# Two blocks in float32 on one core: where the first mixer's tables, weight splits and rotations stand

## The chip, the core and the metric

The kernel runs on one core of a Trainium2 chip. The core's engines each work through a queue of their own in order: TensorE (PE; its weight loads are PEld), VectorE (DVE), ScalarE (ACT), GpSimd (POOL) and SyncE (SP, which here only starts transfers). Semaphores tie the queues together. The metric is the device time of one execution in microseconds (us), and the number to compare is the median over the runs of a kernel.

## What is computed

256 tokens of width 1024 go in float32 through two blocks. The first is feed-forward, attention, feed-forward, each with a norm ahead of it and one behind it; the second has two layers, each a mixer and a feed-forward part.

```
x = x + 0.5 * rmsnorm(swiglu(rmsnorm(x, pre), gate, up, down), post)      # part f1
x = x + rmsnorm(attention(rmsnorm(x, mix_pre)) @ w_out, mix_post)         # part m1, the first mixer
x = x + 0.5 * rmsnorm(swiglu(...), post)                                  # part f2
x = x + ab_mixer(rms_norm(x));  x = x + swiglu(rms_norm(x), ...)          # parts ab, f3
x = x + cd_mixer(rms_norm(x));  x = x + swiglu(rms_norm(x), ...)          # parts cd, f4
return rms_norm(x)
```

The attention of m1 has 8 heads of one kind (group A, two key heads shared by four query heads each, their queries and keys normed per head) and 8 of another (group B). In both, each 64-wide head of queries and keys is rotated: `out = q * cos + swapped(q) * sin`. In group A the norm's gain is multiplied into the cosine and sine tables (`cg`, `sg`), so the rotation is two multiplications, an addition and a multiplication by the norm's `r`.

## The kernel before

**Products.** Each float32 product is made of three fp32r products: an operand is split in a high part (a cast) and a low part (the operand less the cast). Weights come in tiles of 128x1024 (512 KB). `Stream` keeps four raw tiles (`wraw`) and six split ones (`wh`, `wl`): SP starts the load, ACT casts `wraw` to `wh` (L89), and DVE or POOL subtracts to get `wl` (L94). The load of the tile four further on waits until that subtraction is done, since the raw buffer is free only then, and the cast of the tile six further on waits until PE has used the tile. `take` splits ahead to six tiles. Which engine subtracts is written in the code: `ws.pool = (1,)` sends every second tile of a stretch to POOL; empty, all go to DVE.

**Order.** Nothing is reordered: each engine's queue is the order of the program text. `bg` is a list of small pieces of work that `pump` takes from within the products.

**Entry to a part.** `enter` (called by each part but the first through its own) closes the part before for the two halves of 128 tokens, h = 0 and then h = 1: `ew` adds the result to `x` (L406 where there is a norm behind, L409 otherwise), computes the norm of the new `x` (squares on ACT, L336; the power -1/2 on POOL, L344 and L346) and scales it to `xs` (L423). `to_t` transposes `xs` on PE (`tp`, L370), casts it on ACT (`xt`, L373) and subtracts on DVE (`xt`, L378). Two weight tiles are cast and subtracted on the way; the second, `split[1]`, is subtracted on POOL. `first` is the first product, for h = 0 and then h = 1; the transposes of h = 1 stand inside the product of h = 0 (`mid`).

**The first mixer.** `mixer1` makes, in this order on PE: the queries of group A (`gh`), its keys and values (`gemm_a256`, 48 short products, `ga`), the first half of group B's `qb` (`gemm_a`, four tiles, `ga`), then `gemm_a` again with pieces between its tiles: after the second tile the transposes (`tq`, L790) of group A's rotated keys (chunk 4 of `ra`) and of some queries, after the third the other queries, after the fourth the first logits (`step(0)`). A third `gemm_a` has `step(1)` to `step(4)` between its tiles. `step(i)` does the logits of head i (`lg`), the softmax of head i-1 (exponentials on ACT, sum's reciprocal `ls` on DVE, L840, multiplication of `e` by it on POOL, L841), the transposes of head i-3's `e` (`pT`, L849) and the product with the values of head i-4 (`o`).

Behind `gh`, POOL loads `rope`, `gqk` and the mask, makes `cg` and `sg` (L729, eight instructions) and clears `va` and `vb` (L733, four). `rope_a(h)` then does group A's rotation for 10 heads of half h (8 of queries, 2 of keys) in five pieces, with the norm's power on POOL (`rra`, L751). `rope_b(h, eng)` rotates group B's 16 heads of half h in four instructions in a row, for h = 0 on POOL and for h = 1 on DVE (L777, L780 twice, L782):

```
self.ws.pool = (1,)
bank = self.gemm_a()
...
self.flush()
self.ws.pool = ()
bank = self.gemm_a({1: lambda: tr(raf, qta, ((4,), (0, 1))), 2: ..., 3: lambda: step(0)})
...
rope_b(0, nc.gpsimd)
rope_b(1, nc.vector)
```

Of the kernel before, what the change touches and what calls it, by code (L numbers as in the profile page):

```python
# [8 lines left out]
F32 = mybir.dt.float32  # L9
# [22 lines left out]
HH_AT = (352, 352, 96, 352)  # L32
# [156 lines left out]
class Kern:  # L189
# [266 lines left out]
    def enter(self, gname, first):  # L456
# [236 lines left out]

    def mixer1(self, gnext):
        nc, A = self.nc, self.A
        tt = nc.vector.tensor_tensor
        with ExitStack() as st:
# [25 lines left out]
            nc.gpsimd.dma_start(out=rope, in_=A["c_rope"])  # L723
            nc.gpsimd.dma_start(out=gqk, in_=A["gqk"].partition_broadcast(P))
            nc.gpsimd.dma_start(out=mask, in_=A["c_maskb"])
            for h in range(2):
                for tab, i in ((cg, 0), (sg, 1)):
                    for (a, b, g) in ((0, 8, i), (8, 10, 2 + i)):
                        nc.gpsimd.tensor_tensor(  # L729
                            out=tab[:, h, a:b, :], in0=rope[:, h, i:i + 1, :].to_broadcast([P, b - a, 64]),  # L730
                            in1=gqk[:, g:g + 1, :].to_broadcast([P, b - a, 64]), op=ALU.mult)
            for t in va + vb:
                nc.gpsimd.memset(t.bitcast(F32), 0.0)  # L733
            kv = self.gemm_a256()
            for h in range(2):
                nc.vector.tensor_copy(out=fl(qa[:, h, 8:10, :]), in_=kv[:, h, 0:128])
                src = kv[:, h, 128:256].rearrange("p (a w) -> p a w", a=2)
                nc.scalar.copy(out=va[0][:, h, :, 1, :], in_=src)
                tt(out=va[1][:, h, :, 1, :], in0=src, in1=va[0][:, h, :, 1, :].bitcast(F32), op=ALU.subtract)

            def rope_a(h):
                t1 = ap.tile([P, 10, 64], F32, name="t1", tag="pp", bufs=2)
                t2 = ap.tile([P, 10, 64], F32, name="t2", tag="pp", bufs=2)
# [30 lines left out]
            def rope_b(h, eng):
                t2 = ap.tile([P, 16, 64], F32, name="t3", tag="pp", bufs=2)
                cc = rope[:, h, 2:3, :].to_broadcast([P, 16, 64])
                eng.tensor_tensor(out=rb[:, h], in0=qb[:, h], in1=cc, op=ALU.mult)  # L777
                for y in range(2):
                    a, b = slice(32 * y, 32 * y + 32), slice(32 - 32 * y, 64 - 32 * y)
                    eng.tensor_tensor(out=t2[:, :, a], in0=qb[:, h, :, b],  # L780
                                      in1=rope[:, h, 3:4, a].to_broadcast([P, 16, 32]), op=ALU.mult)
                eng.tensor_tensor(out=rb[:, h], in0=rb[:, h], in1=t2, op=ALU.add)  # L782
# [954 lines left out]
```

## Time and profile before

| | before |
| --- | --- |
| median of 3 runs (lowest to highest) | 1124.01 us (1123.45 to 1124.99) |
| the profiled execution | 1124.95 us, of which 1123.2 us are its span |
| busy: PE, PEld | 1094.8 us (97%), 926.4 us |
| busy: DVE, ACT, POOL | 743.5 us (66%), 598.9 us, 357.3 us |
| DMA | 190.83 MB, mean 170 GB/s |

The parts lie in the span about as follows: f1 to 197 us, m1 to 323, f2 to 509, ab to 631, f3 to 826, cd to 932, f4 to the end. The list of PE's waits names who ended an idle stretch of PE; the chain of waits goes back from the last instruction to what released each step; a timeline row gives start, duration, engine, line, operation, output and inputs, and in square brackets the idle time ahead of it and who ended it. A row with xN merges N like instructions in a row.

### The profile page before, as it was taken

The page shows a single profiled execution, that of the slowest core. Times are in us where ns is not written, and L with a number is a line of the kernel's source. Part 1 is how long each engine was busy: PE and PEld are TensorE (multiplying, and loading weights), DVE is VectorE, ACT ScalarE, POOL GpSimd, SP SyncE. Part 2 cuts the span into 40 slices and gives each one's busy share as a digit, 9 for nine tenths or more (in the row PEclk, how much of TensorE's full clock was granted, in tenths as well). Part 3 has the DMA queues.
Part 4 walks back from the last instruction along what each step waited for, and adds up shares of the span by engine and source line. Part 5 has one row for each costly group of instructions (what it writes and reads, how often), then busy time and mean ns, then how long its engine had stood idle before and what let it go on. Part 6 is the DMA issues. An engine that isn't in the chain of part 4 may idle for free.

```text
span 1123.2 us, 16090 instructions
## 1 busy us (share of the span) xinstructions
PE 1094.8 (97%) x5963; PEld 926.4 (82%) x5963; DVE 743.5 (66%) x988; ACT 598.9 (53%) x954; POOL 357.3 (32%) x572
## 2 busy tenths in 40 slices
PE   8999999989999999999989999999999999999997
PEld 5888888767878888887976888888889888888886
DVE  5666566789676665667573677667777656656664
ACT  4567555545655454555664555545452465554553
POOL 2006700655320000004151499999624221000000
PEclk9999999989999999999988999999999999999999
DMA  7765655652047656655621565565554326655651
GB/s 229 251 199 166 209 188 187 211 169 76 20 153 223 201 175 200 211 171 178 204 90 38 187 199 175 190 187 155 183 177 151 131 86 203 196 191 188 215 167 69
DMA packets 130256, 190.83 MB, mean 170 GB/s; under 512 B 6017, under 2 KB 101249, under 8 KB 130178
## 3 DMA queue, kind: packets, MB, share of 16 engines
q1 hardware_dynamic: 129440, 187.72, 52.3%
q0 software_dynamic: 736, 2.08, 0.6%
q8 instruction: 47, 0.77, 0.3%
q14 instruction: 31, 0.25, 0.1%
q10 hardware_dynamic: 2, 0.00, 0.0%
HBM read 188.73 MB, written 1.05 MB: 169 GB/s over the span
## 4 chain that ended last, share of the span: by engine, by line
PE 84%; DVE 6%; POOL 3%; issue 2%; ACT 2%; DMA 1%; SPq 0%; POOLq 0%; DVEq 0%; ACTq 0%
PE gb L535 26%; PE f L523 21%; PE gb L537 13%; PE wo L523 4%; PE gb L523 4%; PE fh L642 3%; PE gh L523 2%; PE ga L523 1%; PE o L869 1%; PE lg L523 1%; PE lt L1100 1%; DVE x L406 1%; DMA wraw<-in_w_first_dram 1%; PE pT L849 1%; PE tp L370 1%
## 5 line engine op out<-in xcount | busy, mean ns | idle before, releaser
L94 DVE TENSOR_TENSOR wl<-wraw,wh 128x1024 fp32r<-128x1024 f32 x323 | 394.0, 1261 | 111.2 <-ACT wh L89 110.7
L535 PE MATMUL gb<-xt,wh 128*128 128x512 f32 x1280 | 439.1, 390 | 0.0
L89 ACT CAST wh<-wraw 128x1024 fp32r<-128x1024 f32 x341 | 345.0, 1047 | 58.1 <-PE f L523 11.4
L537 PE MATMUL gb<-xt,wl 128*128 128x256 f32 x1280 | 353.9, 277 | 0.0
L535 PEld LDWEIGHTS gb<-xt,wh 128*128 128x128 f32 x1280 | 240.3, 188 | 50.6
L537 PEld LDWEIGHTS gb<-xt,wl 128*128 128x128 f32 x1280 | 240.5, 188 | 1.7
L523 PE MATMUL f<-wh,hh 128*128 128x512 f32 x348 | 138.2, 397 | 0.0
L523 PE MATMUL f<-wh,hl 128*128 128x512 f32 x348 | 137.1, 394 | 0.0
L523 PE MATMUL f<-wl,hh 128*128 128x512 f32 x348 | 136.9, 393 | 0.0
L659 ACT COPY sg<-gb 128x256 f32<-128x256 f32 x80 | 29.8, 373 | 140.5 <-PE gb L537 137.2
L660 DVE TENSOR_TENSOR sg<-gb,sg 128x256 f32<-128x256 f32 x80 | 33.4, 423 | 94.4 <-ACT sg L659 94.2
L94 POOL TENSOR_TENSOR wl<-wraw,wh 128x1024 fp32r<-128x1024 f32 x21 | 58.6, 2803 | 86.5 <-ACT wh L89 83.8
L344 POOL TENSOR_TENSOR v<-ss 128x1 f32<-128x1 f32 x22 | 6.2, 281 | 242.0 <-ACT xs L336 180.7
L339 POOL TENSOR_SCALAR ss<-ss 128x1 f32<-128x1 f32 x6 | 2.5, 409 | 244.7 <-ACT xs L336 244.7
L523 PEld LDWEIGHTS f<-wh,hl 128*128 128x128 f32 x348 | 65.3, 188 | 16.8 <-DVE hl L654 0.9
L523 PEld LDWEIGHTS f<-wh,hh 128*128 128x128 f32 x348 | 65.4, 188 | 14.6
L523 PEld LDWEIGHTS f<-wl,hh 128*128 128x128 f32 x348 | 65.4, 188 | 13.3
L523 PE MATMUL gb<-xt,wh 128*128 128x256 f32 x384 | 69.1, 282 | 0.0
L659 ACT COPY su<-gb 128x256 f32<-128x256 f32 x80 | 29.2, 368 | 64.7 <-PE gb L537 64.7
L523 PEld LDWEIGHTS gb<-xt,wh 128*128 128x128 f32 x384 | 59.4, 188 | 0.4
L523 PE MATMUL gb<-xt,wl 128*128 128x256 f32 x192 | 54.3, 283 | 0.0
L523 PE MATMUL wo<-wh,xt 128*128 128x512 f32 x160 | 52.6, 400 | 0.0
(406 smaller groups left out, 1641.9 us busy)
## 6 DMA issues: line engine op xcount, KB each, us to landing
wraw<-in_ffn_w_down_dram SPq DMA_DIRECT2D x88, 512.0 KB, 3.8
wraw<-in_ffn_w_gate_dram SPq DMA_DIRECT2D x80, 512.0 KB, 4.1
wraw<-in_ffn_w_up_dram SPq DMA_DIRECT2D x80, 512.0 KB, 5.6
wraw<-in_ab_w_in_dram SPq DMA_DIRECT2D x20, 512.0 KB, 4.8
wraw<-in_w_qkv_dram SPq DMA_DIRECT2D x18, 512.0 KB, 3.8
wraw<-in_w_first_dram SPq DMA_DIRECT2D x16, 512.0 KB, 3.9
wraw<-in_cd_w_in_dram SPq DMA_DIRECT2D x16, 512.0 KB, 4.5
wraw<-in_w_out_dram SPq DMA_DIRECT2D x8, 512.0 KB, 4.2
```

Of the source, the lines that this page charges most:

```text
L89: self.nc.scalar.copy(out=h, in_=r)
L94: eng.tensor_tensor(out=l, in0=r, in1=h.bitcast(F32), op=ALU.subtract)
L370: nc.tensor.transpose(p[:, j * P:(j + 1) * P], src[:, (b + j) * P:(b + j + 1) * P], self.ident)
L406: nc.vector.scalar_tensor_tensor(out=xv[:, c], in0=t[:, c], scalar=r, in1=xv[:, c], op0=ALU.mult, op1=ALU.add)
L523: self.nc.tensor.matmul(out=out, lhsT=l, rhs=r, start=start and i == 0, stop=stop and i == n - 1)
L535: self.nc.tensor.matmul(out=p, lhsT=wh[:, k % 4, c], rhs=self.x2[:, k, :], start=k == 0, stop=False, skip_group_check=True)
L537: self.nc.tensor.matmul(out=p[:, S:2 * S], lhsT=wl[:, k % 4, c], rhs=self.xh[:, k, :], start=False, stop=k == 7, skip_group_check=True)
L642: nc.tensor.matmul(out=p, lhsT=l, rhs=r, start=n == 0, stop=n == 23)
L659: nc.scalar.copy(out=t[:, c, :], in_=p[:, 1, :])
L660: tt(out=t[:, c, :], in0=p[:, 0, :], in1=t[:, c, :], op=ALU.add)
L849: nc.tensor.transpose(p[:, k * S + h * P:k * S + (h + 1) * P], e[:, h, k * P:(k + 1) * P], self.ident)
L869: nc.tensor.matmul(out=o, lhsT=v, rhs=p, start=i % 2 == 0 and n == 0, stop=i % 2 == 1 and n == 5)
```

## The change

- `enter`: `split[1]` is subtracted on DVE and no longer on POOL, and it stands behind the second `next(e1)` (the update of `x` for h = 1) in place of ahead of the transposes.
- The tiles `rope`, `gqk`, `maskb`, `cg`, `sg`, `va`, `vb` get a pool of their own, opened ahead of f1 and closed behind m1 (`m1_open`). `m1_load` (loads and clears) is hooked to step 5 of f1, `m1_tables(0)` and `m1_tables(1)` to steps 8 and 9. `va` is 5 wide in place of 2x3, with the values at places 1 and 3. Gaps of bytes (`HH_AT`, `gap`) place the tiles.
- `rope_a(h, heads)` takes a slice of the heads: h = 0's eight query heads are rotated at once behind `enter`, ahead of the keys' product; h = 1's eight queries, then the two keys of h = 0 and of h = 1, three pieces each, go through `bg` in the first `gemm_a`.
- `ws.pool` stays empty: no weight tile of the first `gemm_a` is subtracted on POOL.
- `rope_b` runs on DVE for both halves, in four pieces each through `bg` in the third `gemm_a`.

```diff
-HH_AT = (352, 352, 96, 352)
+HH_AT = (512, 352, 96, 352)
...
         next(e1)
-        split[1](nc.gpsimd)
         self.new_xt()
         low = self.to_t(0, xs, self.xh, self.xl)
         next(e1)
+        split[1](nc.vector)
         low()
...
+    def m1_load(self):
+        nc, A = self.nc, self.A
+        nc.gpsimd.dma_start(out=self.rope, in_=A["c_rope"])
+        nc.gpsimd.dma_start(out=self.gqk, in_=A["gqk"].partition_broadcast(P))
+        nc.gpsimd.dma_start(out=self.maskb, in_=A["c_maskb"])
+        for t in self.va + self.vb:
+            nc.gpsimd.memset(t.bitcast(F32), 0.0)
+
+    def m1_tables(self, h):
+        for tab, i in ((self.cg, 0), (self.sg, 1)):
+            for (a, b, g) in ((0, 8, i), (8, 10, 2 + i)):
+                self.nc.gpsimd.tensor_tensor(
...
-            nc.gpsimd.dma_start(out=rope, in_=A["c_rope"])
...
-            for t in va + vb:
-                nc.gpsimd.memset(t.bitcast(F32), 0.0)
...
+            for f in rope_a(0, slice(0, 8)):
+                f()
             kv = self.gemm_a256()
...
-            self.bg += rope_a(0) + rope_a(1)
-            self.pump(3)
+            self.bg += rope_a(1, slice(0, 8)) + rope_a(0, slice(8, 10)) + rope_a(1, slice(8, 10))
...
-            self.ws.pool = (1,)
             bank = self.gemm_a()
...
-            self.ws.pool = ()
...
-            rope_b(0, nc.gpsimd)
-            rope_b(1, nc.vector)
+            self.bg += rope_b(0) + rope_b(1)
...
+                hooks = {j: [step(a), step(b)] for j in (2, 4, 6)} if i == 0 else {}
+                self.m1_open(stm)
+                hooks.update({5: [self.m1_load], 8: [lambda: self.m1_tables(0)], 9: [lambda: self.m1_tables(1)]})
+                self.ffn(pre, "ffn1_post_g", 0.5, nxt, hooks)
```

PE, ACT and SP have the same instructions in the same order as before; DVE's and POOL's queues change. Three places:

DVE at the entry to m1, before, from the scaled `xs` of h = 0 to the low part of h = 1:

```order
L423 SCALAR_TENSOR_TENSOR xs<-x,r,g_mix_pre_g 128x512 x2
L401 TENSOR_TENSOR pt<-f_411,g_ffn_post_g 128x512
L401 TENSOR_TENSOR pt<-f_412,g_ffn_post_g 128x512
L406 SCALAR_TENSOR_TENSOR x<-pt,r,x 128x512 x2
L378 TENSOR_TENSOR xt<-tp,xt 128x4x128 x2
L423 SCALAR_TENSOR_TENSOR xs<-x,r,g_mix_pre_g 128x512 x2
```

The same stretch of DVE now:

```order
L423 SCALAR_TENSOR_TENSOR xs<-x,r,g_mix_pre_g 128x512 x2
L401 TENSOR_TENSOR pt<-f_424,g_ffn_post_g 128x512
L401 TENSOR_TENSOR pt<-f_425,g_ffn_post_g 128x512
L406 SCALAR_TENSOR_TENSOR x<-pt,r,x 128x512 x2
L94 TENSOR_TENSOR wl<-wraw,wh 128x1024
L378 TENSOR_TENSOR xt<-tp,xt 128x4x128 x2
L423 SCALAR_TENSOR_TENSOR xs<-x,r,g_mix_pre_g 128x512 x2
```

One weight subtraction has come between the update of `x` and the low part; the five other entries change in the same way.

DVE ahead of the first transposes `tq` (the low part `qtal` is the first work behind them), before; `t_...` are the rotation's scratch tiles, `ssa` the sums of squares:

```order
L765 TENSOR_TENSOR ra<-t_2178,rra 128x2x4x64
L769 TENSOR_TENSOR ra<-t_2178,rra 128x128
L748 TENSOR_TENSOR t_2184<-qa 128x640
L749 TENSOR_REDUCE ssa<-t_2184 128x10
L754 TENSOR_TENSOR t_2183<-qa,cg 128x640
L94 TENSOR_TENSOR wl<-wraw,wh 128x1024
L758 TENSOR_TENSOR t_2184<-qa,sg 128x20x16 x2
L762 TENSOR_TENSOR t_2183<-t_2183,t_2184 128x640
L765 TENSOR_TENSOR ra<-t_2183,rra 128x2x4x64
L769 TENSOR_TENSOR ra<-t_2183,rra 128x128
L94 TENSOR_TENSOR wl<-wraw,wh 128x1024 x2
L796 TENSOR_TENSOR qtal<-tq,qtah 128x256
```

And now:

```order
L773 TENSOR_TENSOR ra<-t_2254,rra 128x128
L94 TENSOR_TENSOR wl<-wraw,wh 128x1024
L754 TENSOR_TENSOR t_2305<-qa 128x128
L755 TENSOR_REDUCE ssa<-t_2305 128x2
L760 TENSOR_TENSOR t_2304<-qa,cg 128x128
L762 TENSOR_TENSOR t_2305<-qa,sg 128x4x16 x2
L767 TENSOR_TENSOR t_2304<-t_2304,t_2305 128x128
L773 TENSOR_TENSOR ra<-t_2304,rra 128x128
L94 TENSOR_TENSOR wl<-wraw,wh 128x1024 x2
L816 TENSOR_TENSOR qtal<-tq,qtah 128x256
```

What stands last ahead of the transposes is now the rotation of two key heads of h = 1, where it was that of all ten heads of h = 1.

POOL in the same stretch and up to the first multiplications of `e`, before:

```order
L750 TENSOR_SCALAR vva<-ssa 128x10
L751 TENSOR_TENSOR rra<-vva,mhalf 128x10
L94 TENSOR_TENSOR wl<-wraw,wh 128x1024 x2
L750 TENSOR_SCALAR vva<-ssa 128x10
L751 TENSOR_TENSOR rra<-vva,mhalf 128x10
L94 TENSOR_TENSOR wl<-wraw,wh 128x1024
L777 TENSOR_TENSOR rb<-qb,rope 128x1024
L780 TENSOR_TENSOR t_2396<-qb,rope 128x16x32 x2
L782 TENSOR_TENSOR rb<-rb,t_2396 128x1024
L841 TENSOR_TENSOR e<-e,ls 128x512 x8
```

And now:

```order
L756 TENSOR_SCALAR vva<-ssa 128x8
L757 TENSOR_TENSOR rra<-vva,mhalf 128x8
L756 TENSOR_SCALAR vva<-ssa 128x8
L757 TENSOR_TENSOR rra<-vva,mhalf 128x8
L756 TENSOR_SCALAR vva<-ssa 128x2
L757 TENSOR_TENSOR rra<-vva,mhalf 128x2
L756 TENSOR_SCALAR vva<-ssa 128x2
L757 TENSOR_TENSOR rra<-vva,mhalf 128x2
L860 TENSOR_TENSOR e<-e,ls 128x512 x8
```

POOL's three weight subtractions and its half of group B's rotation are gone from here. Its loads and clears (L708 to L712) now follow at the program's start directly on the power of h = 1's first norm (L346), and the eight table instructions (L717) on the last of the small preparations of part f1.

## Rows read from the trace of the kernel before

**Rows 1.** PE's waits: who waited for whom, us in total, times, longest.
```profile
PE lt L1100 <- DVE spl L1092: 3.3, 1, 3.3
PE pT L849 <- POOL e L841: 1.9, 1, 1.9
```

**Rows 2.** Timeline of PE in m1: the transposes of the rotated heads.
```profile
240.14 1.33 PE L790 MATMUL tq<-ident,ra 128*128 128x128 f32 x5 [4.61 <-DVE ra L769]
```

**Rows 3.** Stretches: length, then busy us of PE, PEld, DVE, ACT, POOL; PEclk, DMA share, GB/s.
```profile
8.00:16.00 8.00, 6.27 (x16) 3.55 (x14) 6.41 (x6) 5.35 (x9) 3.42 (x3) 1.00 0.77 257
141.00:157.00 16.00, 16.00 (x88) 13.77 (x87) 9.63 (x13) 8.18 (x12) 0.00 (x0) 1.00 0.60 198
235.20:240.20 5.00, 0.39 (x3) 0.07 (x2) 4.79 (x7) 1.44 (x2) 4.13 (x2) 0.86 0.00 0
240.20:246.00 5.80, 5.80 (x17) 4.74 (x18) 4.31 (x5) 2.01 (x3) 0.00 (x0) 0.54 0.93 326
262.00:264.00 2.00, 0.12 (x1) 0.12 (x2) 1.88 (x5) 1.85 (x6) 1.83 (x2) 1.00 0.79 256
580.00:584.00 4.00, 3.67 (x9) 2.37 (x9) 4.00 (x9) 1.54 (x3) 0.00 (x0) 0.51 0.38 127
```

**Rows 4.** Timeline of DVE at the entry to m1: updates of x, h = 0 and h = 1.
```profile
193.35 1.41 DVE L406 SCALAR_TENSOR_TENSOR x<-pt,r,x 128x512 f32<-128x512 f32 x2 [0.30 <-POOL r L346]
...
199.15 3.38 DVE L406 SCALAR_TENSOR_TENSOR x<-pt,r,x 128x512 f32<-128x512 f32 x2
```

**Rows 5.** Timeline of POOL at that entry: the second tile's subtraction.
```profile
198.87 2.45 POOL L94 TENSOR_TENSOR wl<-wraw,wh 128x1024 fp32r<-128x1024 f32 x1
```

**Rows 6.** Timeline of PE at the entries to m1, f2 and ab.
```profile
203.19 1.19 PE L523 MATMUL gh<-wh,xt 128*128 128x512 f32 x4 [0.38 <-DVE xt L378]
205.13 1.23 PE L370 MATMUL tp<-ident,xs 128*128 128x128 f32 x8 [0.75 <-DVE xs L423]
...
328.89 1.66 PE L642 MATMUL fh<-wh,xt 128*128 128x512 f32 x6 [0.33 <-DVE xt L378]
330.75 1.32 PE L370 MATMUL tp<-ident,xs 128*128 128x128 f32 x8 [0.20 <-DVE xs L423]
...
515.08 1.20 PE L523 MATMUL gh<-wh,xt 128*128 128x512 f32 x4 [0.43 <-DVE xt L378]
517.02 1.23 PE L370 MATMUL tp<-ident,xs 128*128 128x128 f32 x8 [0.75 <-DVE xs L423]
```

**Rows 7.** Timeline of DVE in m1: rotation of group A, and a weight subtraction.
```profile
221.22 0.81 DVE L748 TENSOR_TENSOR t<-qa 128x640 f32<-128x640 f32 x1
...
224.48 1.23 DVE L94 TENSOR_TENSOR wl<-wraw,wh 128x1024 fp32r<-128x1024 f32 x1
...
226.55 2.75 DVE L765 TENSOR_TENSOR ra<-t,rra 128x512 f32<-128x512 f32 x1
...
237.06 2.82 DVE L765 TENSOR_TENSOR ra<-t,rra 128x512 f32<-128x512 f32 x1 [0.17 <-POOL rra L751]
239.80 0.28 DVE L769 TENSOR_TENSOR ra<-t,rra 128x128 f32<-128x128 f32 x1
```

**Rows 8.** Timeline of POOL in m1: last two table instructions, two subtractions, a power.
```profile
213.47 2.71 POOL L729 TENSOR_TENSOR sg<-rope,gqk 128x512 f32<-128x512 f32 x2
...
225.86 5.75 POOL L94 TENSOR_TENSOR wl<-wraw,wh 128x1024 fp32r<-128x1024 f32 x2
...
234.23 2.80 POOL L751 TENSOR_TENSOR rra<-vva,mhalf 128x10 f32<-128x10 f32 x1
```

**Rows 9.** Timeline of ACT in m1: load of a function table, then two casts.
```profile
221.00 1.28 ACT L798 ACT_TABLE_LOAD   x1
222.29 2.16 ACT L89 CAST wh<-wraw 128x1024 fp32r<-128x1024 f32 x2
```

**Rows 10.** Timeline of DVE, then of POOL, in the third product: rotation of group B, first softmax.
```profile
253.97 4.58 DVE L780 TENSOR_TENSOR t<-qb,rope 128x512 f32<-128x512 f32 x2
...
261.89 1.94 POOL L841 TENSOR_TENSOR e<-e,ls 128x512 f32<-128x512 f32 x1 [3.90 <-DVE ls L840]
```

More of the change, by code (lines that the diff above doesn't have):

```diff
@@ L722, in mixer1 @@
             self.gain(gnext)
-            nc.gpsimd.dma_start(out=rope, in_=A["c_rope"])
[L724 to L731, printed above, removed]
@@ L732, in mixer1, with rope_a, a, b @@
-            for t in va + vb:
-                nc.gpsimd.memset(t.bitcast(F32), 0.0)
+            def rope_a(h, heads):
+                n = heads.stop - heads.start
+                w = {}
+                v4 = lambda t: t.rearrange("p n (x y d) -> p (n x) y d", x=2, y=2)
+                src = qa[:, h, heads, :]
+                def a():
+                    t1, t2 = (ap.tile([P, n, 64], F32, name=x, tag="pp", bufs=2) for x in ("t1", "t2"))
+                    ss, v, r = (self.sm.tile([P, 10], F32, name=x, tag=x)[:, 0:n] for x in ("ssa", "vva", "rra"))
+                    w.update(t1=t1, t2=t2, r=r)
+                    tt(out=t2, in0=src, in1=src, op=ALU.mult)
+                    nc.vector.tensor_reduce(out=ss, in_=t2, axis=AX.X, op=ALU.add)
+                    nc.gpsimd.tensor_scalar(out=v, in0=ss, scalar1=1.0 / 64, scalar2=EPS, op0=ALU.mult, op1=ALU.add)
+                    nc.gpsimd.tensor_tensor(out=r, in0=v, in1=self.mhalf[:, 0:n], op=ALU.pow)
+                def b():
+                    tt(out=w["t1"], in0=src, in1=cg[:, h, heads, :], op=ALU.mult)
+                    for y in range(2):
+                        tt(out=v4(w["t2"])[:, :, y, :], in0=v4(src)[:, :, 1 - y, :],
+                           in1=v4(sg[:, h, heads, :])[:, :, y, :], op=ALU.mult)
+                def c():
+                    t1, r = w["t1"], w["r"]
+                    tt(out=t1, in0=t1, in1=w["t2"], op=ALU.add)
+                    if n == 8:
+                        tt(out=ra[:, h, 0:4, :].rearrange("p b (a d) -> p a b d", a=2),
+                           in0=t1.rearrange("p (a b) d -> p a b d", a=2),
+                           in1=r.rearrange("p (a b o) -> p a b o", a=2, o=1).to_broadcast([P, 2, 4, 64]), op=ALU.mult)
+                    else:
+                        tt(out=ra[:, h, 4, :].rearrange("p (a d) -> p a d", a=2), in0=t1,
+                           in1=r.rearrange("p (a o) -> p a o", o=1).to_broadcast([P, 2, 64]), op=ALU.mult)
+                return [a, b, c]
@@ L774, in rope_b @@
[L774 to L782, printed above, removed]
+                nc.scalar.copy(out=va[0][:, h, 1:4:2, :], in_=src)
@@ new lines, in mixer1, with rope_b, b @@
+                tt(out=va[1][:, h, 1:4:2, :], in0=src, in1=va[0][:, h, 1:4:2, :].bitcast(F32), op=ALU.subtract)
+            def rope_b(h):
+                w = {}
+                def a():
+                    w["t"] = ap.tile([P, 16, 64], F32, name="t3", tag="pp", bufs=2)
+                    tt(out=rb[:, h], in0=qb[:, h], in1=rope[:, h, 2:3, :].to_broadcast([P, 16, 64]), op=ALU.mult)
+                def b(y):
+                    a, b = slice(32 * y, 32 * y + 32), slice(32 - 32 * y, 64 - 32 * y)
+                    tt(out=w["t"][:, :, a], in0=qb[:, h, :, b],
+                       in1=rope[:, h, 3:4, a].to_broadcast([P, 16, 32]), op=ALU.mult)
+                def c():
+                    tt(out=rb[:, h], in0=rb[:, h], in1=w["t"], op=ALU.add)
+                return [a, lambda: b(0), lambda: b(1), c]
@@ L881, in heads @@
                     if not hA:
-                        hA.extend(mp.tile([P, 5, S], F32R, name=n, tag=t) for n, t in (("hah", "cg"), ("hal", "sg")))
+                        hA.extend(self.m1p.tile([P, 5, S], F32R, name=n, tag=t) for n, t in (("hah", "cg"), ("hal", "sg")))
                     return [t[:, c, :] for t in hA]
```

53 lines of the change are left out of this document (15 added, 38 removed).

## The prediction

> **What bounds the kernel now.** PE is busy nearly throughout, so only its waits can be won. I read the list of PE's waits first, then timelines of PE where the waits lie, then DVE's, POOL's and ACT's timelines backwards from each wait, and last the stretches with the granted clock. Most waits lie outside the change's reach, such as the 3.3 us of ab's `lt` [rows 1]. Four places lie within it.
>
> At the first transposes of m1, PE waits 4.61 us for `ra`, to 240.14 [rows 2]. It arrives at 240.14 - 4.61 = 235.53. [...] At `pT` PE waits for POOL's first multiplication of `e`, which itself waited 3.90 us for DVE's `ls` [rows 1, 10]. The entries to m1, f2 and ab hold two small waits each for `xt` and `xs` [rows 6].
>
> Behind all four is one pattern. The update of `x` for h = 1 takes 3.38 us, while h = 0's took 1.41; POOL's subtraction starts ahead of it and runs to 201.32 [rows 4, 5]. The multiplication giving `ra` takes 2.75 us beside POOL's two subtractions, the pieces of `rope_b` 4.58 us for two [rows 7, 8, 10]. [...]
>
> **The change part by part.**
>
> Entries. With `split[1]` on DVE, the update should take 1.41 us, 1.97 less; the subtraction adds 1.23 [rows 4, 7]. So `xt` comes 0.7 us earlier and `xs`, which hangs on the squares and POOL's power behind the update, gains nearly all of the 1.97 less what DVE has queued. The waits to cover are 0.38 + 0.75 in m1, 0.33 + 0.20 in f2, 0.43 + 0.75 in ab [rows 6]: 2.84 us. I take them all, with 1.4 (half) as the lower bound: the subtraction now stands ahead of `xt`, `xs` and all who wait for them. It ends by 199.15 + 1.41 + 1.23 = 201.8; PE, which stops at 203.19 - 0.38 = 202.81 for `xt`, has this tile's low part in its last two products before that, at about 202.3. In f3, cd and f4 no wait of this kind is in reach, DVE is free before POOL's power arrives, and I take nothing; the bound is 0.2 us a piece lost.
>
> The wait at `tq`. PE arrives 1.13 earlier, at 234.4. When is `ra` ready? The chain starts at ACT's table load, which ended at 222.28 [rows 9]. It follows the keys' and values' copies, which come earlier by the 1.13 and by about 0.45, since they no longer follow POOL's clears: I take 220.7, the two halves put together. One cast takes 2.16 / 2 = 1.08 [rows 9], so DVE starts on the weight tiles at 221.8. From there its queue is: five subtractions at 1.23, 6.15 us; the rotation of eight heads, whose five whole-width instructions I scale from 640 to 512 columns, 0.81 x 0.8 = 0.65 each, and whose two half-width ones I take at 0.36 each, 4.0 us; two rotations of two heads, each five at 0.28 and two at about 0.2, 3.6 us together [rows 7]. Sum 13.75, so 235.55. To this comes the last power: POOL's for ten heads took 2.80 [rows 8], for two no row of it is there. Its bounds are 0 (it is over while DVE does the other products) and 2.80 less the about 0.8 of DVE's work beside it, 2.0. I take 0.3, near the low end, since two heads are a fifth of ten. `ra` at 235.85, a wait of 1.45 in place of 4.61: 3.16 won; bounds 3.4 and 1.2.
>
> Clock. [...] So the dip goes: 5.80 x (1 - 0.54) = 2.67 us.
>
> The wait at `pT`. The reciprocal `ls` stood behind half of group B's rotation, held up by POOL's half [rows 10]. Uncontended, I estimate 0.65 for a piece of 512 columns and 1.25 for 1024, so 3.8 a half and 7.6 for both; before, one half cost DVE the 4.58 for two pieces and at least 2.5 for the two wide ones, 7.1. DVE's load there hardly rises, and the pieces now come two at a time, so `ls` follows its logits by one subtraction and two pieces, some 3 us, while PE asks for `e` two tiles later. All 1.9 goes. What is late next is DVE itself, whose queue is full there: the differences of `pp` come just as PE wants them. Bounds 0 and 1.9; I take 0.3 lost.
>
> The moved work. The tables cost POOL up to 2.71 for a pair [rows 8], four pairs. In f1 they follow the small preparations, with DVE idle 6.4 of 16 us and POOL idle [rows 3]: nothing, because weights are split six tiles ahead; without that cover, up to 10 us of DVE's time would be in play. The loads wait for nothing, so they start where POOL's queue reaches them, behind its third and last instruction in the stretch from 8 to 16 us [rows 3], not at step 5 of f1. There DMA moves 257 GB/s [rows 3]; 640 KB take 2.5 us. The weights of f1's first step are then under way, but are used only behind f1's first product, most of which is still to come: nothing, bound 2.5. [...]
>
> Sum: 2.84 + 3.16 + 2.67 + 1.9 - 0.3 = 10.3 us. Against the profiled execution's 1124.95 that is 1114.7; it lies 0.94 above the median of 1124.01, so I forecast **1113.7**.
>
> **The rivals.**
>
> [...]
>
> *The loads at the start hurt.* 2.5 us of transfers ahead of the first weights of f1 [rows 3] reach PE in full: 1116.2. Against: the first product covers them.
>
> *DVE becomes the bound of the third product.* POOL's multiplications of `e` read SBUF, 1.94 us each beside DVE [rows 10], and four of them fall beside the eight pieces of `rope_b`. If each holds DVE for its length, DVE is 7.8 us later, PE waits that long, and a wait of that length brings the lower clock [rows 2, 3]: 1113.7 + 7.8 + 2.7 = 1124.2, no change. If POOL reads throughout, so that each of the eight pieces is held as those of one half were, 2.29 in place of 0.65 [rows 10], that is 8 x 1.64 = 13.1 us: 1113.7 + 13.1 + 2.7 = 1129.5, slower. It decides as soon as DVE falls behind PE, since `pp` comes just in time. Against: POOL's queue there holds only the four multiplications, and they wait for DVE as much as DVE for them.
>
> [...]
>
> **How the numbers follow.** What this kernel's measurement can tell from no change is about 0.2%, 2.2 us. Forecast 0.68; keys last 0.13; loads 0.07; DVE the bound without a net change 0.07, slower 0.05. So faster 0.88, same 0.07, slower 0.05. The range takes in the forecast's bounds and the first two rivals: below, 1113.7 less the remaining 1.45 and 0.3 gives 1111.9, and I go to 1111.4; above, 1118.1 and 0.7 for the entries, 1118.8.
>
> **What would show it.** PE's waits after: `xt` and `xs` at the three entries gone or under 0.2; `tq` at 0.5 to 2.5; no `pT`. Stretches of m1 at a granted clock of 1.00 throughout. DVE's timeline: updates of `x` at 1.4 for two, `ra` under 0.8, pieces of `rope_b` at 0.65 and 1.25. The first product of f2 should start about 8.5 us earlier in the span. I am wrong if `tq` waits over 3 us, if a clock under 1.00 shows in m1, if PE waits for `pp` or `e` in the steps, or if f1 is longer.

## The result, and the profile after

The changed kernel takes **1113.49 us** (median of 4, 1109.38 to 1114.61) where the kernel before took 1123.73 beside it; the ratio is 0.990, 95% interval 0.9874 to 0.9926. Measured a second time it took 1113.63, ratio 0.9907 (0.9894 to 0.9920). The forecast was 1113.7, range 1111.4 to 1118.8. The profiled execution is one of 1114.61 us with a span of 1112.8, against 1123.2 before.

The list of PE's waits of the changed kernel (who waited for whom, us in total, times, longest):

```profile
PE lt L1116 <- DVE spl L1108: 3.3, 1, 3.3
...
PE fh L642 <- ACT xt L373: 1.5, 3, 1.0
PE tp L370 <- DVE xs L423: 1.2, 3, 0.6
PE o L888 <- DVE pp L871: 1.2, 2, 0.7
...
PE tq L810 <- DVE ra L773: 0.9, 1, 0.9
```

Against [rows 1, 2] the wait at `pT` is gone and `tq` has fallen from 4.61 to 0.9. The product `o`, which waited 0.6 us for `pp` in one place before, now waits 1.2 in two. The 3.3 us in ab are untouched.

**The entries.** The timelines of DVE and of PE at the entry to m1 answer to [rows 4] and [rows 6]:

```profile
199.21 1.41 DVE L406 SCALAR_TENSOR_TENSOR x<-pt,r,x 128x512 f32<-128x512 f32 x2
200.53 1.22 DVE L94 TENSOR_TENSOR wl<-wraw,wh 128x1024 fp32r<-128x1024 f32 x1
```

```profile
203.75 1.23 PE L370 MATMUL tp<-ident,xs 128*128 128x128 f32 x8
```

The update of `x` for h = 1 takes 1.41 us in place of 3.38, the subtraction 1.22, and the transposes of h = 1 start at 203.75 without a wait, where they started at 205.13 behind one of 0.75. In f2 and ab the waits of h = 1 are gone as well. At f2 the first transposes (those of h = 0) now wait 0.62 where they waited 0.32.

**The first transposes.** PE's timeline, then POOL's and DVE's behind it, at the place of [rows 2]:

```profile
235.08 0.77 PE L810 MATMUL tq<-ident,ra 128*128 128x128 f32 x5 [0.93 <-DVE ra L773]
```

```profile
234.01 0.70 POOL L757 TENSOR_TENSOR rra<-vva,mhalf 128x2 f32<-128x2 f32 x1
```

```profile
234.74 0.29 DVE L773 TENSOR_TENSOR ra<-t,rra 128x128 f32<-128x128 f32 x1 [0.39 <-POOL rra L757]
```

The power of two heads takes 0.70 (ten took 2.80, [rows 8]), DVE waits 0.39 for it, and PE waits 0.93. Behind the wait the clock stays up; the stretches that answer to [rows 3] (length, then busy us of PE, PEld, DVE, ACT, POOL; PEclk, DMA share, GB/s):

```profile
141.00:157.00 16.00, 16.00 (x88) 13.77 (x87) 12.70 (x13) 8.20 (x12) 8.82 (x6) 1.00 0.63 198
235.20:238.00 2.80, 2.80 (x16) 2.38 (x17) 2.80 (x4) 1.92 (x3) 0.00 (x0) 1.00 0.46 181
238.00:244.00 6.00, 6.00 (x31) 4.70 (x30) 4.47 (x7) 3.79 (x6) 0.00 (x0) 1.00 0.91 269
```

The first of the three is the part of f1 where the tables now stand: POOL is busy for 8.82 us where it did nothing, DVE for 12.70 in place of 9.63, and PE for all 16.

**Group B's rotation.** DVE, then POOL, in the third product, at the place of [rows 10]:

```profile
245.86 0.69 DVE L796 TENSOR_TENSOR t<-qb,rope 128x512 f32<-128x512 f32 x1
...
248.65 1.53 DVE L796 TENSOR_TENSOR t<-qb,rope 128x512 f32<-128x512 f32 x1
...
253.35 2.06 DVE L792 TENSOR_TENSOR rb<-qb,rope 128x1024 f32<-128x1024 f32 x1
```

```profile
247.69 1.94 POOL L860 TENSOR_TENSOR e<-e,ls 128x512 f32<-128x512 f32 x1 [12.99 <-DVE ls L859]
252.39 1.94 POOL L860 TENSOR_TENSOR e<-e,ls 128x512 f32<-128x512 f32 x1 [2.76 <-DVE ls L859]
256.96 1.04 POOL L860 TENSOR_TENSOR e<-e,ls 128x512 f32<-128x512 f32 x1 [2.63 <-DVE ls L859]
```

A piece of 512 columns takes 0.69 alone and 1.53 beside a multiplication of `e`; one of 1024 takes 1.22 alone (at 244.72) and 2.06 beside one. The first two multiplications of `e` take 1.94, the third 1.04. The reciprocal comes in time, and no `pT` waits.

### The profile page after: what moved, and what is told of

Same layout as the page of the kernel before. It is cut to its first block, busy times and chain, and to the rows that moved or that the text cites. A ratio compares the mean times of both kernels' runs of the same rounds, so it can differ in the third digit from the quotient of the medians.

```text
span 1112.8 us, 16111 instructions
## 1 busy us (share of the span) xinstructions
PE 1091.2 (98%) x5963; PEld 924.5 (83%) x5963; DVE 742.7 (67%) x1013; ACT 600.0 (54%) x954; POOL 325.8 (29%) x563
## 3 DMA queue, kind: packets, MB, share of 16 engines
HBM read 188.73 MB, written 1.05 MB: 171 GB/s over the span
## 4 chain that ended last, share of the span: by engine, by line
PE 87%; DVE 6%; issue 2%; ACT 2%; POOL 2%; DMA 1%; SPq 0%; POOLq 0%; DVEq 0%; ACTq 0%
PE gb L535 26%; PE f L523 21%; PE gb L537 13%; PE wo L523 4%; PE gb L523 4%; PE fh L642 4%; PE gh L523 3%; PE ga L523 1%; DVE wl L94 1%; PE tp L370 1%; DMA wraw<-in_w_first_dram 1%; PE lt L1116 1%; PE lg L523 1%; PE o L888 1%; PE M L1376 1%
## 5 line engine op out<-in xcount | busy, mean ns | idle before, releaser
L94 DVE TENSOR_TENSOR wl<-wraw,wh 128x1024 fp32r<-128x1024 f32 x332 | 405.4, 1262 | 107.7 <-ACT wh L89 106.8
L94 POOL TENSOR_TENSOR wl<-wraw,wh 128x1024 fp32r<-128x1024 f32 x12 | 33.2, 2785 | 86.1 <-ACT wh L89 83.4
```

What stands on the lines that cost most here:

```text
L94: eng.tensor_tensor(out=l, in0=r, in1=h.bitcast(F32), op=ALU.subtract)
```

## A measure finer than the median

The parts were compared in a stretch of the trace that repeats well: from the first transposes of m1 to those of f2, from there to those of ab, and from there to the transposes `lt` of ab (start times from PE's timelines). Only the parts before `lt` are used, for a reason that the last section shows: behind it the granted clock differs from execution to execution (a loss of 3.4 to 8.5 us in ab). All times are in us. Each ratio is to runs of the kernel before taken beside it, whose medians were 1123.73 to 1124.87.

| kernel | median (runs) | ratio to before, interval | m1 | f2 | ab to `lt` | sum |
| --- | --- | --- | --- | --- | --- | --- |
| before | 1123.73 (4) | | 125.71 | 186.16 | 70.94 | 382.8 |
| changed | 1113.49 (4) | 0.990 (0.9874 to 0.9926) | 117.14 | 184.96 | 69.46 | 371.6 |
| changed, again (e5) | 1113.63 (4) | 0.9907 (0.9894 to 0.9920) | 117.49 | 184.96 | 69.49 | 371.9 |
| entries undone (e1) | 1116.65 (6) | 0.9935 (0.9918 to 0.9952) | 118.66 | 186.14 | 70.94 | 375.7 |
| three tiles on POOL (e2) | 1118.79 (6) | 0.9950 (0.9936 to 0.9965) | 122.35 | 184.97 | 69.48 | 376.8 |
| old `rope_b` (e3) | 1116.52 (6) | 0.9927 (0.9912 to 0.9942) | 119.48 | 184.96 | 69.48 | 373.9 |
| table load early (e4) | 1113.11 (6) | 0.9898 (0.9882 to 0.9913) | 116.34 | 184.95 | 69.47 | 370.8 |
| before, split alone (e6) | 1118.83 (6) | 0.9960 (0.9946 to 0.9974) | 119.77 | 186.23 | 70.97 | 377.0 |
| wait + six (e7) | 1120.39 (5) | 0.9969 (0.9957 to 0.9981) | 122.20 | 184.95 | 69.49 | 376.6 |
| `e` on ACT (e8) | 1119.67 (12) | 0.9966 (0.9952 to 0.9980) | 127.49 | 184.98 | 69.48 | 382.0 |
| before, three edits (e9) | 1114.88 (5) | 0.9919 (0.9902 to 0.9936) | 117.84 | 184.98 | 69.44 | 372.3 |
| tables in m1 (e10) | 1121.16 (8) | 0.9970 (0.9958 to 0.9983) | 124.38 | 184.97 | 69.55 | 378.9 |
| best tried (e11) | 1113.76 (4) | 0.9901 (0.9883 to 0.9918) | 117.51 | 184.98 | 69.44 | 371.9 |
| wait + three (e12) | 1116.07 (4) | 0.9925 (0.9900 to 0.9950) | 118.71 | 185.01 | 69.49 | 373.2 |

The f2 column takes two values only, 186.2 with the old entry and 185.0 with the new one, and ab two as well. Each row's stretches come from one execution, and m1 repeats less well: it is 117.14 and 117.49 in the two of the changed kernel (the mean, 117.3, is what the experiments below are held against). So 0.5 us in m1 is not told from chance by one execution. From before to after the sum falls by 11.1 (10.9 in e5), and the whole span by 10.4.

## The experiments

### The change undone, one edit at a time (e1 to e3)

First the entry, with the second tile on GpSimd at its old place:

```diff
         next(e1)
+        split[1](nc.gpsimd)
         self.new_xt()
         low = self.to_t(0, xs, self.xh, self.xl)
         next(e1)
-        split[1](nc.vector)
         low()
```

> The changed kernel with one edit undone: the second weight tile at each entry is subtracted on GpSimd again, at its old place. As forecast (entries worth 2.84 us): 1113.5 + 2.8 = 1116.3. What the trace of the changed kernel suggests instead: both waits went in m1 (1.13) and the second one in f2 and ab (0.20 and 0.75), but f2's first wait grew from 0.33 to 0.62 and ab's stayed near 0.4, so 1.8 to 1.9: 1115.4. Rival, that the entries are worth nothing because PE would wait later for DVE anyway (tq is 0.9 now and would simply be shorter): 1113.5 + 0.9 or less. In the trace the update of x for h = 1 takes 3.4 us for two again and tp waits 0.75 in m1 and ab.

Measured: the sum of the stretches rises by 4.0 us, 1.3 in m1, 1.2 in f2, 1.5 in ab. The entries are worth more than either figure (the lower one missed that in the changed kernel all six waits of h = 1 are gone). PE's timeline at the entry to f2 says why, first in this kernel, then in the changed one:

```profile
321.23 1.66 PE L642 MATMUL fh<-wh,xt 128*128 128x512 f32 x6 [0.32 <-DVE xt L378]
323.09 1.32 PE L370 MATMUL tp<-ident,xs 128*128 128x128 f32 x8 [0.20 <-DVE xs L423]
324.16 1.17 PE L642 MATMUL fh<-wh,xt 128*128 128x512 f32 x4
```

```profile
319.88 1.54 PE L642 MATMUL fh<-wh,xt 128*128 128x512 f32 x6
321.25 1.04 PE L370 MATMUL tp<-ident,xs 128*128 128x128 f32 x8
322.05 1.21 PE L642 MATMUL fh<-wh,xt 128*128 128x512 f32 x4
```

Six products that follow a stop end 1.66 us after their start, and where none comes before them the next group starts 1.37 after theirs (321.25 - 319.88); the eight transposes need 324.16 - 323.09 = 1.07 to the next start against 322.05 - 321.25 = 0.80. So each stop costs nearly 0.3 us besides the idle time shown in brackets; why, no run shows. Six stops went: 6 x 0.28 = 1.7 on top of 2.84 of idle time, less the 0.3 that the first transposes of f2 now wait longer, is 4.2, near the 4.0 measured.

Next, GpSimd gets weight tiles of the first `gemm_a` again:

```diff
+            self.ws.pool = (1,)
             bank = self.gemm_a()
...
             self.flush()
+            self.ws.pool = ()
```

> The changed kernel with two weight tiles of the first gemm_a subtracted on GpSimd again. [...] Rival (GpSimd takes work off DVE): DVE loses two subtractions of 1.22, the wait of 0.9 goes: 1112.6.

Measured: 5.05 us more in m1 and nothing in f2 and in ab up to `lt`. The trace has three weight tiles on POOL, as the kernel before had, and not the two that the expectation names. PE now waits twice at `tq`, 2.98 and 1.52, and in DVE's and POOL's timelines two multiplications last longer than the weight subtraction beside them:

```profile
227.78 2.93 DVE L769 TENSOR_TENSOR ra<-t,rra 128x512 f32<-128x512 f32 x1 [0.46 <-POOL rra L757]
...
233.29 2.49 DVE L773 TENSOR_TENSOR ra<-t,rra 128x128 f32<-128x128 f32 x1
```

```profile
227.72 2.44 POOL L94 TENSOR_TENSOR wl<-wraw,wh 128x1024 fp32r<-128x1024 f32 x1
...
233.24 2.40 POOL L94 TENSOR_TENSOR wl<-wraw,wh 128x1024 fp32r<-128x1024 f32 x1
```

The multiplication of 128 columns, 0.29 us in the changed kernel, takes 2.49: it starts 0.05 behind the subtraction on POOL and ends 0.14 behind it. The one of 512 columns, 0.69 in e6 and e10, takes 2.93: it starts 0.06 behind the subtraction and ends 0.55 behind it. Behind the waits the granted clock is 0.54 over 3.50 us (length, busy us, PEclk, DMA share, GB/s as above); the 0.50 to which it falls in e3 and e7 is called the lower level below:

```profile
238.00:241.50 3.50, 3.50 (x12) 2.97 (x11) 3.50 (x5) 1.90 (x3) 0.00 (x0) 0.54 0.89 342
```

The longer waits (4.50 in place of about 1.1) and the clock (3.50 x 0.46 = 1.6) together make up the 5.05.

The third edit undone is group B's rotation:

```diff
...
-            self.bg += rope_b(0) + rope_b(1)
+            rope_b(0, nc.gpsimd)
+            rope_b(1, nc.vector)
```

> The changed kernel with group B's rotation as before: h = 0 in one row on GpSimd, h = 1 in one row on DVE. As forecast: the wait for pT comes back at 1.9, with the waits for pp (1.2 now, 0.6 before) down by 0.6: 1113.5 + 1.3 = 1114.8, up to 1115.4 if pp keeps its waits. Rival (DVE is the bound of this stretch, so that half the work on GpSimd is as good): within 0.3 of 1113.5. A wait over 3 us there with a clock of 0.5 behind it would give over 1118.

Measured: 2.2 us more in m1. The wait for `pT` is back at its old length, and here the clock falls to 0.50 behind it. In the kernel before it did not (1.00); the stretch from 262 to 264 in [rows 3] is that wait itself, so the first row below has what followed it there, and the others are this kernel's:

```profile
264.00:265.00 1.00, 1.00 (x7) 0.92 (x8) 1.00 (x1) 1.00 (x5) 1.00 (x1) 1.00 0.47 74
```

```profile
256.69 0.98 PE L861 MATMUL pT<-ident,e 128*128 128x128 f32 x4 [1.96 <-POOL e L853]
```

```profile
257.00:260.00 3.00, 3.00 (x10) 2.45 (x9) 2.97 (x6) 3.00 (x9) 2.80 (x2) 0.50 0.77 212
```

From 257 to 260 the lower level alone costs 3.00 x 0.5 = 1.5. Without it the old rotation would be dearer by some 0.7 only (an estimate, 2.2 - 1.5); part of what it loses at `pT` it has back at `pp`, for which the changed kernel waits 1.2 and this one 0.7.

### The change built up from the kernel before (e6, e9)

```diff
-            self.ws.pool = (1,)
             bank = self.gemm_a()
```

> The kernel before with one edit of the change: no weight tile of the first gemm_a is subtracted on GpSimd. [...] Rival (the placing of the tables and the cut of the rotation did it all, the split nothing): no change, or 1 us more. Second rival (the split alone was enough): wait under 2, no lower clock, 5 us less.

Measured: the second rival. One line takes 5.9 us off m1 (125.71 to 119.77), about half of what the whole change takes:

```profile
237.73 0.77 PE L790 MATMUL tq<-ident,ra 128*128 128x128 f32 x5 [1.16 <-DVE ra L769]
...
259.00 0.66 PE L849 MATMUL pT<-ident,e 128*128 128x128 f32 x4 [1.91 <-POOL e L841]
```

```profile
238.00:244.00 6.00, 6.00 (x32) 4.96 (x31) 5.37 (x7) 3.93 (x6) 0.14 (x1) 1.00 0.86 287
```

`tq` waits 1.16 with ten heads a piece and the tables made in m1. DVE's timeline shows why one line is enough. In the kernel before, each of POOL's three subtractions held up a short multiplication: those of 2.75 and 2.82 in [rows 7] and, between them, one of 128 columns. That one first, then two of the three in this kernel:

```profile
229.22 2.54 DVE L769 TENSOR_TENSOR ra<-t,rra 128x128 f32<-128x128 f32 x1
```

```profile
228.57 0.69 DVE L765 TENSOR_TENSOR ra<-t,rra 128x512 f32<-128x512 f32 x1
229.19 0.28 DVE L769 TENSOR_TENSOR ra<-t,rra 128x128 f32<-128x128 f32 x1
```

The three take 0.69, 0.28 and 0.68 here, 6.5 us less together, and DVE takes over three subtractions of up to 1.22: some 2.8 of the 3.45 by which the wait falls. The ten-head power of 2.80 [rows 8], which I had thought a limit, ends at 235.87, ahead of DVE's own queue.

> The kernel before with three edits of the change alone: the entry's second subtraction on DVE behind the update, no weight tile of the first gemm_a on GpSimd, group B's rotation in pieces on DVE. Tables, loads and clears stay in m1, group A's rotation keeps its ten heads a piece. Theory, from the earlier runs (undone one by one, the three cost 4.0, 5.1 and 2.2 us from the entry to m1 to the transposes lt of ab, 11.3 of the 11.1 that the whole change won there): this kernel is the changed kernel, 1113.6 within 0.6, ratio to before 0.990 to 0.991, tq waits 0.9 to 1.6. Rival (the tables' new place and the rotation ahead of the keys do their share at tq): tq waits 2 to 4 us and the time is 1115 to 1118.

This kernel is the one before with the edit of `enter`, the line of e6 and the pieces of `rope_b`. Measured: 372.3 in the sum of the stretches against 371.6 and 371.9; `tq` waits 1.60, `pp` is waited for 1.4. The tables' new place and the cut of group A's rotation are together worth about 0.5 us at most: two executions of the changed kernel differ by 0.35 in m1, and the ratios, 0.9919 here, 0.9900 and 0.9907 there, have overlapping intervals.

### The tables back in m1, with the new rotation (e10)

```diff
             self.gain(gnext)
+            self.m1_load()
+            for h in range(2):
+                self.m1_tables(h)
...
-                hooks.update({5: [self.m1_load], 8: [lambda: self.m1_tables(0)], 9: [lambda: self.m1_tables(1)]})
```

> The changed kernel with loads, clears and tables made behind the first product of m1 again; the rotation of eight query heads stands ahead of the keys as in the changed kernel. Theory (the move of the tables pays only for this rotation's place): DVE waits there for cg and sg of h = 0, made on GpSimd behind 4.3 us of clears, until about 211 to 213 in place of 209, its four weight subtractions and the copies of the keys come 2 to 4 us later, and tq waits 2.5 to 4.5 with the lower clock behind it from about 3 on: 1115 to 1119. Rival (DVE's idle time of 3.4 us between 207 and 222 takes it up): 1113.6. That the loads at the start of f1 hurt would show as up to 0.1 us less here ahead of m1.

Measured: 7.1 us more in m1, beyond what either theory gave. POOL's timeline, then DVE's, then PE's:

```profile
213.61 2.17 POOL L717 TENSOR_TENSOR sg<-rope,gqk 128x512 f32<-128x512 f32 x2
215.87 0.20 POOL L759 TENSOR_SCALAR vva<-ssa 128x8 f32<-128x8 f32 x1
216.15 1.67 POOL L760 TENSOR_TENSOR rra<-vva,mhalf 128x8 f32<-128x8 f32 x1
```

```profile
217.85 0.69 DVE L772 TENSOR_TENSOR ra<-t,rra 128x512 f32<-128x512 f32 x1 [3.66 <-POOL rra L760]
218.46 4.62 DVE L94 TENSOR_TENSOR wl<-wraw,wh 128x1024 fp32r<-128x1024 f32 x4
```

```profile
219.73 0.50 PE L523 MATMUL ga<-wl,xt 128*128 128x512 f32 x1 [2.71 <-DVE wl L94]
...
240.32 0.77 PE L813 MATMUL tq<-ident,ra 128*128 128x128 f32 x5 [2.11 <-DVE ra L776]
```

I had looked at the tables as something that DVE reads. What costs more is that the norm's power is queued behind all eight table instructions on POOL: DVE waits 3.66 us for it with four weight subtractions behind, and PE runs out of split weights, a wait of 2.71 that the kernel before does not have. Both waits have the lower clock behind them (0.50 from 221 to 224 and from 242 to 244); the clock's shortfall, summed over both, is 3.4 us, which with the 2.71 and the 1.0 that `tq` waits longer makes up the 7.1. So the eight heads ahead of the keys need the tables made earlier, but by e9 the two edits together gain hardly anything over leaving both out.

### The wait and the clock (e7, e12)

In the last `ra`'s piece for h = 1, with N = 6 and N = 3:

```diff
+                        if h == 1:
+                            t3 = ap.tile([P, 2, S], F32, name="t5", tag="e")
+                            for _ in range(N):
+                                tt(out=fl(t3), in0=fl(qa[:, 0, 0:8, :]), in1=fl(qa[:, 0, 0:8, :]), op=ALU.mult)
```

> The changed kernel with six more multiplications of 512 columns on DVE ahead of the last ra, results unused: 6 x 0.6 = 3.6 us, of which the 0.39 that DVE waits there for the power cover a part, so tq waits 0.9 + 3.2 = 4.1. Theory (a wait of this length brings the lower clock behind it, 2.67 us in the kernel before): 1113.5 + 3.2 + 2.7 = 1119.4, and the clock is 0.5 for about 5 us behind the wait. Rival (the clock fell in the kernel before for another reason, such as the small transposes or DMA there): 1116.7 at a clock of 1.00.

> The changed kernel with three more multiplications of 512 columns on DVE ahead of the last ra (six were 4.7 us of waiting): tq waits 1.1 to 1.3 plus 1.5, so 2.4 to 2.8, between the 1.9 of pT that left the clock at 1.00 in the kernel before and in the run with the split alone, the 1.96 of pT with the clock at 0.50 behind it in the run with the old rotation of group B, and the 3.3 of ab. If the wait's length decides, and the limit lies near 2: 1113.6 + 1.5 + 1.7 = 1116.8 with the clock at 0.50 for 3.4 us. If it lies near 3, or if what PE does around the wait decides as well: 1115.1, clock 1.00.

Measured: `tq` waits 4.68 and 2.50. First the six, then the three; each with the stretch behind the wait:

```profile
238.26 1.33 PE L814 MATMUL tq<-ident,ra 128*128 128x128 f32 x5 [4.68 <-DVE ra L777]
```

```profile
238.20:241.00 2.80, 2.73 (x9) 2.45 (x10) 2.80 (x5) 1.74 (x3) 0.00 (x0) 0.50 0.14 29
```

```profile
234.36 0.76 PE L814 MATMUL tq<-ident,ra 128*128 128x128 f32 x5 [2.50 <-DVE ra L777]
```

```profile
234.40:240.00 5.60, 5.60 (x29) 4.71 (x30) 4.98 (x7) 3.52 (x6) 0.00 (x0) 1.00 0.62 185
```

With six the lower level lies behind the wait, and m1 grows by 4.9 us (122.20 against a mean of 117.3), of which 3.6 is the added wait. The clock's share is so 1.3, half of what it was behind nearly the same wait in the kernel before (2.67, [rows 2, 3]). With three m1 grows by 1.4, the added wait alone, at a clock of 1.00, the second case of the expectation. Both medians lie further off, by 6.8 and 2.4; in the profiled executions cd is longer by 3.4 to 4.1 and ab shorter by 1.7 to 2.1 than in the two of the changed kernel (last section).

### The multiplications of `e` on ACT (e8)

```diff
+                if i < 4:
+                    for h in range(2):
+                        nc.scalar.mul(e[:, h, :], e[:, h, :], l[:, h:h + 1])
+                else:
                     nc.gpsimd.tensor_tensor(out=e, in0=e, ...
```

> The changed kernel with the multiplication of e by the reciprocal sum on ACT in place of GpSimd for the first four heads, those that run beside group B's rotation. Theory (GpSimd's reading of e holds DVE there): the two pieces of 1.53 and 2.06 take 0.69 and 1.22, DVE is 1.7 us less behind, and the 1.2 us that PE waits for pp go wholly or for the greater part: 1112.3 to 1112.9. Rival (DVE is behind by its own work): pp is waited for as before, 1113.5. Second rival: ACT, which then waits for DVE's reciprocal in its queue, brings casts and exponentials late: 1114 to 1116.

Measured: 10.2 us more in m1, the second rival and beyond its price. The theory about DVE was right as far as DVE goes: all eight pieces of `rope_b` take 0.68 or 0.69 and 1.22. But ACT now stands still for the reciprocal, with the next cast and exponentials behind it, and DVE waits for those in turn. ACT's timeline, then PE's:

```profile
247.59 0.91 ACT L862 ACTIVATE e<-e,ls 128x256 f32<-128x256 f32 x2 [2.86 <-DVE ls L859]
...
253.46 0.91 ACT L862 ACTIVATE e<-e,ls 128x256 f32<-128x256 f32 x2 [3.11 <-DVE ls L859]
```

```profile
266.98 0.80 PE L892 MATMUL o<-pp,vah 128*128 128x256 f32 x2 [3.22 <-ACT pp L874]
```

```profile
263.00:279.00 16.00, 12.78 (x55) 10.93 (x53) 10.60 (x23) 8.20 (x23) 3.12 (x3) 0.50 0.14 34
```

Behind the two waits of 1.50 and 3.22 PE runs at the lower level for 16 us, in a stretch where it has many short products and transposes.

### Two attempts to do better (e4, e11)

```diff
             kv = self.gemm_a256()
+            nc.scalar.preload_act_table_set("natural_log_exp_and_others")
...
-            nc.scalar.preload_act_table_set("natural_log_exp_and_others")
             self.bg += rope_a(1, slice(0, 8)) + ...
```

> The changed kernel with ACT's load of the exponential table (1.28 us) moved ahead of the copies of keys and values, into 2.10 us in which ACT waits. If the chain to tq starts at that load, the cast behind it and all of DVE's queue come up to 1.3 us earlier, and the 0.9 us at tq goes: 1112.6. Rival: the cast after next waits for its DMA anyway (2.02 us), or the last power on GpSimd is bound by its own chain: no gain, 1113.5.

And with the pieces of `rope_b` grouped as well:

```diff
-            self.bg += rope_b(0) + rope_b(1)
+            two = lambda f, g: lambda: (f(), g())
+            p = rope_b(0) + rope_b(1)
+            self.bg += [p[0], two(p[1], p[2]), p[3], two(p[4], p[5]), p[6], p[7]]
```

> The changed kernel with two more edits: ACT's table load ahead of the copies of keys and values (as in the fourth run, which took 0.9 to 1.3 us off tq), and group B's pieces taken 3, 3, 2 and 0 a tile in place of 2 each, so that none stands ahead of the second difference pp. Theory: tq no longer waits, and of the 1.2 us that PE waits for pp the later 0.6 goes, perhaps both: 1113.6 - 1.1 - 0.6 to 1.2 = 1111.3 to 1111.9. Rival (three pieces in a row hold up ls and so e, or POOL's e holds longer pieces): pT or pp wait as much or more, 1112.5 or above.

Measured: in the profiled execution of e4 `tq` does not wait and m1 is 1.0 us shorter; in that of e11, which is the same up to there, `tq` waits 1.65. Both make the first cast behind the copies of keys and values at 218.63; ACT's second cast tells the difference, e4 first:

```profile
220.48 1.05 ACT L89 CAST wh<-wraw 128x1024 fp32r<-128x1024 f32 x1 [0.80 <-DMA wraw<-in_w_qkv_dram]
```

```profile
222.01 1.05 ACT L89 CAST wh<-wraw 128x1024 fp32r<-128x1024 f32 x1 [2.33 <-DMA wraw<-in_w_qkv_dram]
```

With the table load out of the way the next limit is the arrival of the weight tile, which came 1.5 us later in one execution than in the other; why, the runs do not show. The regrouping took the wait for `pp` from 1.2 to 0.9. Both medians, 1113.11 and 1113.76, are not to be told from the changed kernel's: neither beats it.

## Why the prediction was right, and where its steps were off

**What bounds the kernel.** Right: PE's waits at the four places, what a stop costs besides (nearly 0.3 us), and the lower clock behind one of them (0.54 over 5.80 us, [rows 3]) account for what was won. The first product of f2 starts 8.5 us earlier, as forecast (324.59 to 316.08). Of the signs listed two did not come: PE does wait for `pp` in the steps (1.2 us), which was named as a sign of being wrong, and two pieces of `rope_b` are longer than forecast. In m1 the granted clock is 1.00 throughout, and f1 is as long as before (190.4).

**Entries, 2.84: too small, 4.0 measured.** The working held row for row (1.41 for the update, no wait at `xt` and `xs`). The term was mis-sized because only idle time was counted; the nearly 0.3 us that PE loses besides at each stop is in the durations of [rows 6], which all belong to groups behind a stop, but no group without one stood beside them. In f3 the bound came true: its stretch is 195.1 us with the old entry (before, e1, e6) and 195.3 with the new one.

**The wait at `tq`, 3.16: right in size, wrong in part of its reason.** The queue was followed well: DVE starts its weight tiles at 221.51 (221.8 forecast), and the last `ra` ends at 235.03 (235.85); the last power cost DVE 0.39 (0.3 taken). The waits of 0.93 and 1.28 are in place of 1.45. (The lower bound of 1.2 does not follow from its own terms: with a power of 2.0 `ra` comes at 237.55, PE waits 3.15, and 1.46 is won.) But the working credits the cut of the rotation and the move of the tables with it. The split alone brings `tq` to 1.16 (e6), and with the new entry and without the rest `tq` waits 1.60 (e9), so that the rest adds about 0.5.

**Clock, 2.67: right here, an estimate that no row had shown.** In e6, where the wait fell by 3.45 and m1 by 5.9, the clock's share is about 2.5. The 5.80 us at 0.54 were there to be won [rows 3], but no row and no run has a wait of 1.45; that all of it would go behind such a wait was my estimate. The row of [rows 3] from 262 to 264 is the wait at `pT` itself; what follows that wait is at 1.00 too. In the term's place the runs showed 1.00 behind the 0.93 that came and behind waits of 1.16 and 1.91 (e6), 1.60 (e9), 1.65 (e11) and 2.50 (e12), and 0.50 behind one of 1.96 (e3) and one of 2.11 (e10). Nor is the size of the term set by the wait: behind one of 4.68 the clock cost 1.3 (e7), behind the 4.61 of the kernel before 2.67.

**`pT`, 1.9 - 0.3: too large.** The wait went and the reciprocal came in time, but PE waits 1.2 for `pp` where it waited 0.6. From e6 to e9 m1 falls by 1.93; 1.3 of it is the entry, and `tq` waits 0.44 longer, so the pieces are worth 1.93 - 1.3 + 0.44 = 1.1 at most where the clock stays up (the 0.7 from e3 is the other estimate).

**The moved work, nothing: right.** DMA carried 263 GB/s from 16 to 24 us where it had carried 189, no new PE wait came of it, and the first product `gb` of f1 starts at 26.25 against 26.20.

That the median came within 0.2 us of the forecast is in part luck. The entries gave 1.2 more and `pT` 0.5 to 0.9 less than forecast; up to `lt` 11.1 was won in place of 10.3, and the profiled execution loses 0.8 again behind it, 0.2 in f3 and 0.6 in cd. The 0.6 is not the change's: in its second execution (e5) cd takes 105.4 us, as in the kernel before.

**The rivals.** *Keys last* (0.13): in kind yes, the last `ra` still ends the wait and DVE still waits for its power, but for 0.39 us and not for the upper bound of 2.0. The 1118.1 in the range is the forecast with such a power and the lower clock put back (1.7 and 2.7); no run shows these terms: the power of two heads took 0.70, `tq` waited 0.93, and the clock behind it was 1.00. *Loads at the start*: no. *DVE becomes the bound*: in kind yes, a piece is longer beside two of the four multiplications of `e`, by 0.84 us each (1.53 - 0.69, 2.06 - 1.22), not 1.94 each; beside a third a weight subtraction is longer by 0.48 (1.70 against 1.22), and the fourth falls beside the differences `pp`, of 0.67, and `vbl`, of 0.68 (all sixteen of `pp` take 0.67 to 0.69). DVE is then 2.2 us late, of which PE feels about 0.6 at `pp`. The price in the rival, 7.8, was over three times too high, because it let every multiplication hold DVE for 1.94. Nearly half of that is POOL's own: the first one, of 1.94, starts at 247.69 beside a weight subtraction that DVE had begun at 247.53, and the third, with no weight subtraction begun ahead of it, takes 1.04.

## What to carry to other kernels

Before sharing out work by how full the queues are, look at which instructions of another engine are longer beside it: one line, three weight tiles moved from GpSimd to a DVE that seemed the busier engine, made about half of this gain (5.9 of 11.1), because beside each a short DVE instruction on the path took 2.5 to 2.8 us, and without them 0.28 to 0.69. Count a stop of TensorE as its idle time and what it loses besides (nearly 0.3 us here), read as the distance between the starts of the next two groups with and without the stop. And when several edits come together, build up from the kernel before as well as undoing them: undoing the tables alone showed 7 us, building up without them and the new rotation 0.5 at most.

## What the runs showed of the hardware beyond that

**The lower clock does not follow from the wait alone.** In m1 a wait of 2.50 left the clock at 1.00 (e12) where waits of 1.96 (e3) and 2.11 (e10) had the lower level behind them. In cd PE waits 1.05 and 0.42 us for `ed` in the changed kernel, and 1.08 and 0.42 in e6, in the same code (the second wait ends at 862.46 and at 863.81). The stretch from 866 on, first in the changed kernel, then in e6:

```profile
866.00:876.00 10.00, 8.91 (x48) 7.23 (x48) 7.42 (x16) 3.89 (x8) 3.94 (x4) 1.00 0.19 67
```

```profile
866.00:876.00 10.00, 10.00 (x41) 9.21 (x41) 4.01 (x12) 0.00 (x0) 0.82 (x2) 0.54 0.29 102
```

The second is almost wholly at the lower level (0.54 in the mean); cd takes 109.4 us there and 106.0 in the changed kernel (105.4 in e5 and in the kernel before). e7 and e12 look like e6 (0.58 from 865 to 870 and from 860 to 865). In ab the wait of 3.3 us is followed by the lower level in the kernel before, the changed one, e1 and e3 to e12, but for different lengths: the loss (1 less the granted clock, summed over the stretch) is 8.5 us in the changed kernel and the one before, 5.1 in e1 and 3.4 in e6, though ab's instructions are the same but for the entry, and 5.1 in e11, whose instructions in ab are those of the changed kernel. That makes a median of four runs uncertain by a microsecond or two here, and it probably explains the one run of the changed kernel at 1109.38, whose mean granted clock was 0.994 against 0.990 to 0.991 in the others; no trace of that run was kept, but the profiled execution of e11 is such a low one (1111.54, clock 0.994, where the other three are 1113.68 to 1114.07): ab is 3.1 us shorter in it than in the changed kernel's (117.3 against 120.3). What decides it was not settled.
